# A hybrid encoder step on one Trainium2 core: the sliding window's first weights and columns cast before the gates end, and two scores ahead of the last memory values

## The chip, the cores and the metric

The kernel runs on one core of a Trainium2 chip. A core has five engines that run side by side, each taking its own instructions in order and waiting on semaphores: TensorE (PE, matrix products, with its weight loads shown apart as PEld), VectorE (DVE), ScalarE (ACT), GpSimd (POOL) and SyncE (SP), which here only issues transfers. Any of the last three can also issue transfers, and such an issue stands in that engine's own row of instructions. The metric is the device time of one execution in microseconds; less is better. Three executions of the kernel before took 2241.95, 2242.7 and 2243.11 us, so the median is 2242.7 us.

## The reference

One layer of a chunk-causal streaming encoder is computed for a prompt of 1024 tokens and a sample of 64, which the kernel holds side by side as 1088 columns. Cut to what the change touches:

```python
rq, rk, rv, rg, sq, sk, sv, ga, gb = split(rms_norm(x, g_attn) @ w_in)
ret_o = retention(rq, rk, rv)                       # 4 heads, chunkwise recurrence
a = (rms_norm(ret_o) * silu(rg)) @ w_ret_out        # branch A
# branch B: window of the own chunk of 64 and the two before, 16 heads, 2 key heads
s = sq @ sk.T * 64 ** -0.5 + bias                   # scores, masked
m = maximum(max(s), sink)
e = exp(s - m)
b = (e / (sum(e) + exp(sink - m)) @ sv) @ w_swa_out
x += (sigmoid(ga) * a + sigmoid(gb) * b) @ w_mix_out
mk, mv = (rms_norm(mem, g_mem) @ w for w in (w_mk, w_mv))   # 256 memory tokens, 4 heads
x += cross_attention(rms_norm(x, g_cross), mk, mv)
x += swiglu(rms_norm(x, g_ffn))
```

Everything is float32. The matrix products keep that precision with two parts: an operand is split into a high part (a cast to the engine's shorter format) and a low part (the rest), and a product is the sum of high times high, high times low and low times high.

## The kernel before

Activations lie with the 1024 model columns on partitions, eight blocks of 128, and tokens along the row. Two sets of eight large places in on-chip memory (`rings`, each place 2 x 1088 numbers a partition) hold the split operands of a stage, and are handed on from stage to stage; what doesn't fit goes through DRAM buffers named `d_...`. A weight block arrives by a transfer into a place named `raw`, its high part is cast by ACT (`split`, L123) and its low part subtracted by DVE (L124), both into a place named `wq`. `mm3` (L149 to L151) issues the three matmuls of a split product. The large projections run as a Strassen scheme with seven products per pair of weight blocks instead (L205, L206, L208), whose partial sums DVE collects.

The program is one stream of statements which a scheduler spreads over the engines: it simulates times, and orders each engine's instructions by them, within limits that the code gives (`issue_after`, `high_priority`). Memory comes from pools, and a tile that takes a place used before waits for the last use of that place.

The stages, with their time in the trace of before:

- `project_phase` (to about 816 us): all projections and the retention. It ends with twelve pairs of gate columns: four of `w_ga`, four of `w_rg`, four of `w_gb`. For each half of the tokens DVE adds the last partial sum (L571), multiplies by the norm (L577), ACT applies the sigmoid or silu (L580), and a transfer writes the result to `d_gate`, on ACT's queue for `w_ga` and `w_gb` and on SP's for `w_rg`. Between the pairs come steps of `memory_phase`, the keys and values of the memory tokens for three of the four value heads, whose weights have three places of their own, `mw`.
- `mix_phase` (about 816 to 1024 us): the sliding window, with `w_ret_out` as filler. `swa` goes through 34 half chunks. In a loop step it weighs the values of half i - 1 (L1006), computes the scores of half i + 2 (L948), and transposes the probabilities of half i (`turn`, L990). The softmax of a half lies between: DVE adds the bias and takes maxima (L958 or L961, L963 to L968), ACT takes four exponentials (L970) and one for the sink, DVE inverts the sum, POOL scales (L976). The scores have one PSUM place, so each waits until DVE has read the scores before it. What the window leaves of PE's time is filled by half products of `filler`: the operands `ret` (the gated retention, reloaded from `d_gate` in three column chunks of 384, 384 and 320 and split), the last memory value head (`w_mv[3]`), and then 8 x 3 pieces of `w_ret_out`, each in two halves of 12 matmuls and closed by a multiplication with the gate (L1103). Of these `fill` places four half products after the first scores, none after the second, 40 over the 34 loop steps and 8 at the end.
- then `merge_swa`, the cross attention, and the feed-forward part to the end.

Weights come from one pool with five `wq` places and two `raw` places during `project_phase`, and from a second one with six and two behind it. The operands `ret`, the queries, keys and bias (`swin`) and the weights `w_mv[3]` are all loaded by code that stands behind the projection.

## Time and profile before

| | us |
|---|---|
| median of three runs | 2242.7 (2241.95 to 2243.11) |
| profiled execution, its own time | 2244.47 |
| its span in the trace | 2242.7 |
| PE busy | 2168.9 (97%) |
| DVE busy | 1596.0 (71%) |
| ACT busy | 885.4 (39%) |
| POOL busy | 692.1 (31%) |

The profile's page gives the busy time of each engine, and the granted clock of TensorE over the span (PEclk, mean 0.988 of full speed). Its other views cut the trace: a table of windows gives each engine's busy time in each stretch, with clock and share of the transfer engines; the waits list what an engine's instructions waited for; the timeline of one engine lists its instructions with, in brackets, the idle time ahead of each and what ended it. In the names, `pq<-T,wq 128*128 128x272` is a matmul from `T` and `wq` into `pq`; `x8` counts instructions that lie together, and their busy time may overlap. An engine's queue (SPq, ACTq) is where its transfers are issued; the columns of such a row give the start and the time up to the last of its issues, waits included.

### The profile page before, as it was taken

Reading aid. Unit: us, or ns where it says so; the run is one execution under the profiler, and the core shown is the slowest. Engines: PE = TensorE matmul, PEld = TensorE weight load, DVE = VectorE, ACT = ScalarE, POOL = GpSimd, SP = SyncE. Lnnn points to the kernel's source line nnn. Section 1 sums busy time; section 2 is a strip of 40 time slices with the busy share of each in tenths; the row PEclk is TensorE's granted clock in tenths of the full one; section 3 lists DMA queues with packets and bytes.
Section 4 is the critical chain, followed back from the end, with each engine's and each line's share of the span. In section 5 each row is a group of like instructions: output and inputs, shape, how many; then the busy total and the mean of one; then the engine's idle time right before and its main releaser. Section 6 shows DMA issues by size and latency. Waiting matters only on the chain.

```text
span 2242.7 us, 41756 instructions
## 1 busy us (share of the span) xinstructions
PE 2168.9 (97%) x16434; PEld 2105.3 (94%) x16434; DVE 1596.0 (71%) x2655; ACT 885.4 (39%) x1897; POOL 692.1 (31%) x466
## 2 busy tenths in 40 slices
PE   8899999999999989999999999999999999999986
PEld 8899999999999977779999998999999999999986
DVE  7986878666687667776455556668777677778587
ACT  7333333435444355554133333333323222344243
POOL 1441533342253112220000000014556555434462
PEclk9999999999999999999999999999999999999998
DMA  5533445443445475326443111422333332475233
GB/s 193 163 108 114 118 124 136 133 126 114 167 151 181 150 229 163 114 69 211 132 152 101 64 46 59 138 89 88 121 129 102 102 120 90 147 267 184 85 98 108
DMA packets 182599, 290.86 MB, mean 130 GB/s; under 512 B 40290, under 2 KB 110850, under 8 KB 182402
## 3 DMA queue, kind: packets, MB, share of 16 engines
q1 hardware_dynamic: 177794, 279.26, 39.3%
q10 hardware_dynamic: 4608, 8.91, 1.1%
q8 instruction: 130, 2.13, 0.4%
q14 instruction: 67, 0.55, 0.1%
HBM read 196.95 MB, written 91.16 MB: 128 GB/s over the span
## 4 chain that ended last, share of the span: by engine, by line
PE 79%; DVE 11%; DMA 5%; issue 2%; ACT 2%; POOL 1%; SPq 0%; DVEq 0%; ACTq 0%; POOLq 0%
PE pq L208 15%; PE pq L206 15%; PE pq L205 15%; PE pd L149 8%; PE pd L151 8%; PE pd L150 8%; DVE wq L124 2%; PE pout L1006 1%; DMA hl<-d_op 1%; PE pp L990 1%; PE pss L948 1%; DVE T L124 1%; DVE B L124 1%; DVE xg L1294 1%; DMA qs<-d_qkv 1%
## 5 line engine op out<-in xcount | busy, mean ns | idle before, releaser
L124 DVE TENSOR_TENSOR wq<-raw,wq 128x512 fp32r<-128x512 f32 (+1 forms) x505 | 448.8, 893 | 125.2 <-ACT wq L123 122.0
L123 ACT CAST wq<-raw 128x512 fp32r<-128x512 f32 (+1 forms) x505 | 307.5, 614 | 568.0 <-PE pq L208 259.1
L205 PE MATMUL pq<-T,wq 128*128 128x272 f32 x1832 | 492.9, 289 | 6.8 <-DVE u L252 3.6
L206 PE MATMUL pq<-T,wq 128*128 128x272 f32 x1832 | 493.0, 289 | 0.0
L206 PE MATMUL pq<-B,wq 128*128 128x272 f32 x1592 | 428.9, 289 | 9.1 <-DVE B L124 9.1
L205 PE MATMUL pq<-B,wq 128*128 128x272 f32 x1592 | 427.1, 289 | 0.2 <-ACT B L123 0.2
L208 PE MATMUL pq<-T,wq 128*128 128x272 f32 x1832 | 384.5, 290 | 3.4 <-DVE wq L124 3.4
L183 POOL TENSOR_TENSOR raw<-raw 128x512 f32<-128x512 f32 (+1 forms) x59 | 80.1, 1357 | 897.2 <-DVE rs_r L291 485.7
L205 PEld LDWEIGHTS pq<-T,wq 128*128 128x128 f32 x1832 | 346.1, 189 | 7.9 <-DVE u L252 3.7
L206 PEld LDWEIGHTS pq<-T,wq 128*128 128x128 f32 x1832 | 345.9, 189 | 0.3 <-issue 0.3
L208 PE MATMUL pq<-B,wq 128*128 128x272 f32 x1592 | 333.9, 290 | 0.0
L206 PEld LDWEIGHTS pq<-B,wq 128*128 128x128 f32 x1592 | 300.4, 189 | 11.0 <-DVE B L124 10.7
L205 PEld LDWEIGHTS pq<-B,wq 128*128 128x128 f32 x1592 | 300.2, 189 | 0.9 <-issue 0.4
L208 PEld LDWEIGHTS pq<-T,wq 128*128 128x128 f32 x1832 | 291.2, 190 | 4.6 <-DVE wq L124 3.8
L208 PEld LDWEIGHTS pq<-B,wq 128*128 128x128 f32 x1592 | 252.9, 190 | 0.5 <-issue 0.3
L252 DVE TENSOR_TENSOR u<-pq,u 128x544 f32<-128x544 f32 x177 | 127.6, 721 | 109.7 <-PE pq L208 109.2
L186 POOL TENSOR_TENSOR raw<-raw 128x512 f32<-128x512 f32 (+1 forms) x59 | 85.5, 1449 | 127.3 <-DVE wq L124 124.7
L976 POOL TENSOR_TENSOR t<-t,den 128x768 f32<-128x768 f32 (+2 forms) x34 | 47.9, 1408 | 170.7 <-DVE den L974 44.4
L571 DVE TENSOR_TENSOR stage<-pq,u 128x544 f32<-128x544 f32 x112 | 80.4, 718 | 26.4 <-PE pq L208 25.4
L184 POOL TENSOR_TENSOR raw<-raw 128x512 f32<-128x512 f32 (+1 forms) x59 | 87.3, 1480 | 3.7
L1461 POOL TENSOR_TENSOR y<-u,y 128x544 f32<-128x544 f32 x38 | 62.6, 1656 | 72.6 <-DVE y L1459 50.5
L189 POOL TENSOR_TENSOR raw<-raw 128x512 f32<-128x512 f32 (+1 forms) x59 | 83.3, 1412 | 4.4
(373 smaller groups left out, 4677.0 us busy)
## 6 DMA issues: line engine op xcount, KB each, us to landing
hl<-d_op SPq DMA_DIRECT2D x85, 272.0 KB, 4.6
d_qkv<-stage SPq DMA_DIRECT2D x44, 272.0 KB, 2.3
d_op<-stage SPq DMA_DIRECT2D x44, 272.0 KB, 2.4
d_op<-ht SPq DMA_DIRECT2D x44, 272.0 KB, 3.3
raw<-w_gate SPq DMA_DIRECT2D x22, 512.0 KB, 3.5
raw<-w_up SPq DMA_DIRECT2D x22, 512.0 KB, 3.6
d_gate<-stage ACTq DMA_DIRECT2D x32, 272.0 KB, 2.7
raw<-w_down SPq DMA_DIRECT2D x16, 512.0 KB, 4.2
```

Of the source, the lines that this page charges most:

```text
L123: self.last_cast = self.nc.scalar.copy(hi, src).ins
L124: return self.nc.vector.tensor_tensor(out=lo, in0=src, in1=hi.bitcast(F32), op=ALU.subtract).ins
L149: mm(ps, wh, xh, start=start, stop=False)
L150: mm(ps, wh, xl, start=False, stop=False)
L151: self.last_mm = mm(ps, wl, xh, start=False, stop=stop).ins
L184: tt(out=a21, in0=a21, in1=a22, op=add)
L186: tt(out=a11, in0=a22, in1=a11, op=sub)
L189: tt(out=a12, in0=a12, in1=a11, op=sub)
L205: mm(ps[:, c, :HC], w[:, 0, ks], x[:, 0, cs], start=start, stop=False)
L206: mm(ps[:, c, :HC], w[:, 0, ks], x[:, 1, cs], start=False, stop=False)
L208: self.last_mm = mm(ps[:, c, :HC], w[:, 1, ks], x[:, 0, c * HC:(c + 1) * HC], start=False, stop=stop).ins
L252: add = lambda out, a, b: nc.vector.tensor_tensor(out=out, in0=a, in1=b, op=ALU.add)
```

## The change

It has six parts.

1. One weights pool with five `wq` and two `raw` places serves the whole program. The sixth `wq` place is a pool of its own, opened ahead of the fourth pair of `w_ga`, and used by every sixth operand from there on. For this the pool of the Strassen sums is closed and opened again behind it, and the two pools of the gate and memory stage are opened there and no longer ahead of `w_sk`. `mw` has two places and no longer three.
2. `memory_phase` also loads and splits `w_mv[3]`, ahead of the last gate pairs' end.
3. `begin_swa`, called as the last statement of `project_phase`, issues the loads of keys, first queries and bias, the loads of the first chunk of the `ret` operands, and ACT's casts of these and of `w_ret_out[0]`. Their low parts (`first_low`, 10 subtractions) follow behind the maxima of the second scores.
4. The PSUM pool of the filler is opened from the other end, so that other banks come to the scores.
5. The second scores stand ahead of the memory values. Six half products follow them: four of the values, and the two halves of the first piece of `w_ret_out`. 38 are spread over the loop, 8 follow at the end. The pieces go chunk by chunk for the first two weight blocks, and the second and third chunks of the operands are loaded and split by fours during half products 2, 3, 5 and 7 of `w_ret_out`.
6. The last gate pair's four stores, and the four stores of the last memory values, are issued by POOL. They stood on ACT's queue and on SP's. The queries of chunks 4 to 7 are loaded in loop step 2, no longer with the first scores.

The counts of matmuls, casts, subtractions, exponentials and transfers are the same as before. The diff, cut to its core:

```diff
     def new_op(self):
-        return self.wp.tile([P, 2, 512], F32R, tag="wq", bufs=self.wbufs, name="wq")
+        self.turns += self.sixth is not None
+        if self.turns and self.turns % 6 == 0:
+            return self.sixth.tile([P, 2, 512], F32R, tag="wq", bufs=1, name="wq")
+        return self.wp.tile([P, 2, 512], F32R, tag="wq", bufs=5, name="wq")
...
-                with self.weights(5):
-                    self.project_phase()
-                with self.weights(6):
-                    with self.plain_psum():
...
+                self.left = sctx.enter_context(ExitStack())
+                self.sixth, self.turns = None, 0
+                self.wp = self.left.enter_context(tc.tile_pool(name="weights", bufs=2, reuse_waits="tile"))
+                self.project_phase()
+                with self.plain_psum(side="right"):
...
-        room = lambda: mp.tile([P, 1024], F32, tag="mw", bufs=3, name="mw")
+        room = lambda: mp.tile([P, 1024], F32, tag="mw", bufs=2, name="mw")
...
-        for h in range(H - 1):
+        for h in range(H):
             us = [self.unit(io["w_mv"][h, i], 4, 256, room) for i in range(2)]
+            if h == H - 1:
+                self.first_units = us
+                yield
+                return
...
                 for m in range(0, KT, 2):
-                    store = nc.scalar.dma_start if idx else self.store
+                    if (idx, m) == (1, 6):
+                        fctx.close()
+                        self.sixth = self.left.enter_context(tc.tile_pool(name="sixth", bufs=1, reuse_waits="tile"))
+                        self.sums_pool(ctx)
+                        op = ...
+                        mp = ...
+                        memory = self.memory_phase(mp)
+                    store = nc.gpsimd.dma_start if (idx, m) == (2, KT - 2) else nc.scalar.dma_start if idx else self.store
...
+            next(memory)
+            self.begin_swa()
...
                 pieces = self.filler()
-                yield [pieces] * 4
                 yield []
-                count, steps, done = 48 - 8, 2 * 17, 0
+                yield [pieces] * 6
+                count, steps, done = 48 - 10, 2 * 17, 0
...
+    def begin_swa(self):
...
+        with tc.high_priority():
+            self.tokens(self.kT, 0, "ckT")
+            self.load_queries(self.qTs, 0)
+            for e in range(2):
...
+                self.loaded = self.load(self.bias[e * 64:(e + 1) * 64], src)
+        self.rets = [self.rings[1].tile(f"ret{k}", slot=i) for k, i in enumerate((0, 1, 4, 5, 6, 7, 2, 3))]
+        self.marks = []
+        self.first_loads()
...
+    def first_loads(self):
...
+        raw = self.unit_raw(self.io["w_ret_out"][0], KT)
+        for k in range(KT):
+            a = self.ld()[:, :n]
+            with self.tc.issue_after(after):
+                self.last_operand = self.load(a, self.d_gate[0][k, :, c0:c0 + n])
+            r = self.rets[k][:, :, c0:c0 + n]
+            self.first.append((a, r[:, 0], r[:, 1]))
+            nc.scalar.copy(r[:, 0], a)
+        qs = [self.new_op() for i in range(2)]
+        for i, q in enumerate(qs):
+            a = raw[:, i * 512:(i + 1) * 512]
+            nc.scalar.copy(q[:, 0], a)
+            self.first.insert(i * 5, (a, q[:, 0], q[:, 1]))
...
+    def first_low(self):
+        with self.tc.issue_after(self.marks[-1][0]):
+            for a, hi, lo in self.first:
+                self.nc.vector.tensor_tensor(out=lo, in0=a, in1=hi.bitcast(F32), op=ALU.subtract)
+
+    def later_operands(self, c0, n, ks):
+        a, b = self.marks[-1]
+        with self.tc.issue_after(a), self.tc.issue_after(b):
+            for k in ks:
+                x = self.ld()[:, :n]
+                with self.tc.issue_after(self.last_operand):
+                    self.last_operand = self.load(x, self.d_gate[0][k, :, c0:c0 + n])
+                self.split(x, self.rets[k][:, 0, c0:c0 + n], self.rets[k][:, 1, c0:c0 + n])
...
-            for c0, n in CH:
-                operands(c0, n)
+            ld, rets = self.ld, self.rets
+            self.first_low()
...
-                self.store(self.d_mv[h, :, t, :], o)
-                self.store(io["o_mv"][t * P:(t + 1) * P, h * 256:(h + 1) * 256], o)
+                nc.gpsimd.dma_start(self.d_mv[h, :, t, :], o)
+                nc.gpsimd.dma_start(io["o_mv"][t * P:(t + 1) * P, h * 256:(h + 1) * 256], o)
...
+            order = [(m, c) for c in range(3) for m in range(2)] + [(m, c) for m in range(2, KT) for c in range(3)]
+            halves = [range(4), range(4, KT)]
+            extra = {2: (1, 0), 3: (1, 1), 5: (2, 0), 7: (2, 1)}
+            step = 0
+            for m, c in order:
...
+                for ps in self.pieces(u, rets, c0, n):
+                    if step in extra:
+                        i, j = extra.pop(step)
+                        self.later_operands(*CH[i], halves[j])
+                    step += 1
```

Where this moves instructions, four rows of the program show it. Names carry a tile number, and `swin` tiles 9709 and 9710 of the change are keys and queries, as 9704 and 9705 are before; the change's line numbers differ (L205, L206, L208 are L209, L210, L212, and L948 is L942).

PE before, where the last gate pair ends:

```order
L205 MATMUL pq<-T_304,wq 128x272
L206 MATMUL pq<-T_304,wq 128x272
L208 MATMUL pq<-T_304,wq 128x272 x2
L948 MATMUL pss<-swin_9704,swin_9705 128x64 x4
L149 MATMUL pd<-wq,ms_7465 128x256
L150 MATMUL pd<-wq,ms_7465 128x256
```

PE with the change, at the same place:

```order
L209 MATMUL pq<-T_304,wq 128x272
L210 MATMUL pq<-T_304,wq 128x272
L212 MATMUL pq<-T_304,wq 128x272 x2
L942 MATMUL pss<-swin_9709,swin_9710 128x64 x8
L153 MATMUL pd<-wq,ms_7472 128x256
L154 MATMUL pd<-wq,ms_7472 128x256
```

Eight score matmuls, of two halves, stand where four stood; the 48 matmuls of the memory values follow in both.

DVE before, from the last addition of the gates on (`wq<-raw` are the low parts of `w_mv[3]`):

```order
L571 TENSOR_TENSOR stage_553<-pq,u_9489 128x544
L577 TENSOR_TENSOR stage_553<-stage_553,rstd 128x544
L124 TENSOR_TENSOR wq<-raw,wq 128x512 x4
L961 SCALAR_TENSOR_TENSOR t<-pss,swin_9706 128x2x64 x2
L963 TENSOR_REDUCE nm<-t 128x4
L964 TENSOR_TENSOR nm<-nm,sinks 128x4
L124 TENSOR_TENSOR ret_9758<-swin_9707,ret_9758 128x384
L965 TENSOR_SCALAR nm<-nm 128x4
L124 TENSOR_TENSOR ret_9759<-swin_9707,ret_9759 128x384
L968 TENSOR_TENSOR es<-sinks,nm 128x4
L124 TENSOR_TENSOR ret_9760<-swin_9707,ret_9760 128x384
L124 TENSOR_TENSOR ret_9761<-swin_9707,ret_9761 128x384
```

DVE with the change, from the same addition on:

```order
L577 TENSOR_TENSOR stage_553<-pq,u_9496 128x544
L583 TENSOR_TENSOR stage_553<-stage_553,rstd 128x544
L955 SCALAR_TENSOR_TENSOR t<-pss,swin_9711 128x2x64 x2
L957 TENSOR_REDUCE nm<-t 128x4
L958 TENSOR_TENSOR nm<-nm,sinks 128x4
L959 TENSOR_SCALAR nm<-nm 128x4
L962 TENSOR_TENSOR es<-sinks,nm 128x4
L955 SCALAR_TENSOR_TENSOR t<-pss,swin_9711 128x2x64 x2
L957 TENSOR_REDUCE nm<-t 128x4
L967 TENSOR_TENSOR den<-den,es 128x4
L958 TENSOR_TENSOR nm<-nm,sinks 128x4
L968 RECIPROCAL den<-den 128x4
```

The four subtractions for `w_mv[3]` no longer stand between the gates and the scores' bias addition (L961, now L955); the `ret` subtractions no longer stand among the maxima, but behind the second scores' maxima, two rows further on than the last row shown.

ACT before, from the end of the last gate pair on (L580 is the sigmoid, L666 its store, L970 the exponentials):

```order
L580 ACTIVATE stage_553<-stage_553 128x544
L666 DMA d_gate_83<-stage_553 128x544
L580 ACTIVATE stage_553<-stage_553 128x544
L666 DMA d_gate_83<-stage_553 128x544
L123 CAST wq<-raw 128x512 x4
L123 CAST ret_9758<-swin_9707 128x384
L123 CAST ret_9759<-swin_9707 128x384
L123 CAST ret_9760<-swin_9707 128x384
L970 ACT_TABLE_LOAD
L970 ACTIVATE t,den<-t,nm 128x64 x4
L123 CAST ret_9761<-swin_9707 128x384
L972 ACTIVATE es<-es 128x4
```

ACT with the change, from the sigmoid ahead of the last three on (L586 is the sigmoid, L1075 and L1079 are the casts of `first_loads`, L964 the exponentials):

```order
L1075 CAST ret_9725<-swin_9712 128x384
L1075 CAST ret_9726<-swin_9712 128x384
L586 ACTIVATE stage_553<-stage_553 128x544
L1079 CAST wq<-raw 128x512
L1075 CAST ret_9727<-swin_9712 128x384
L1075 CAST ret_9729<-swin_9715 128x384
L1075 CAST ret_9730<-swin_9715 128x384
L586 ACTIVATE stage_553<-stage_553 128x544
L1079 CAST wq<-raw 128x512
L586 ACTIVATE stage_553<-stage_553 128x544
L964 ACT_TABLE_LOAD
L964 ACTIVATE t,den<-t,nm 128x64 x4
```

The casts of the first operands stand among and ahead of the sigmoids, no longer behind them; the stores are gone, and the exponentials of the first two halves follow directly.

POOL before, from its last sum in the gates on (L976 scales the probabilities):

```order
L184 TENSOR_TENSOR raw<-raw 128x512
L186 TENSOR_TENSOR raw<-raw 128x512
L189 TENSOR_TENSOR raw<-raw 128x512
L976 TENSOR_TENSOR t<-t,den 128x4x64 x2
L976 TENSOR_TENSOR t<-t,den 128x4x128 x2
L976 TENSOR_TENSOR t<-t,den 128x768 x30
```

POOL with the change, at the same place (L970 scales, L676 stores the gates, L1135 and L1136 the memory values):

```order
L190 TENSOR_TENSOR raw<-raw 128x512
L193 TENSOR_TENSOR raw<-raw 128x512
L676 DMA d_gate_83<-stage_553 128x544 x4
L970 TENSOR_TENSOR t<-t,den 128x4x64
L1135 DMA d_mv<-swin_9715 128x256
L1136 DMA o_mv<-swin_9715 128x256
L970 TENSOR_TENSOR t<-t,den 128x4x64
L1135 DMA d_mv<-swin_9715 128x256
L1136 DMA o_mv<-swin_9715 128x256
L970 TENSOR_TENSOR t<-t,den 128x4x128 x2
L970 TENSOR_TENSOR t<-t,den 128x768 x30
```

Four issues of stores stand ahead of the first scaling, two ahead of the second, and two ahead of the third.

More of the change, by code (lines that the diff above doesn't have):

```diff
@@ L890, in swa @@
             mm = nc.tensor.matmul
[L892 to L913 removed]
+            flat, kT, bias, qTs, sinks = self.flat, self.kT, self.bias, self.qTs, self.sinks
+            vT = flat[5][:, :KC]
+            vts = [flat[4][:, i * P:(i + 1) * P] for i in range(17)] + [flat[0][:, KC + i * P:KC + (i + 1) * P] for i in range(3)]
             def keep():
@@ L941, in scores @@
                 ks, j0, nk = keys(c)
[L942 removed]
+                if hf == 0 and c % 4 == 0 and 0 < c < 13:
                     self.load_queries(qTs, c + 4)
@@ L967, in scores @@
                 es = sw.tile([P, 2, 2], F32, tag="es", name="es")
-                nc.vector.tensor_tensor(out=es, in0=snk, in1=nm, op=ALU.add)
+                ready = nc.vector.tensor_tensor(out=es, in0=snk, in1=nm, op=ALU.add).ins
                 for v, i in units:
@@ new lines, in tokens, with ld @@
+    def tokens(self, dst, i, cache):
+        self.load(dst[:, :SEQ], self.d_skv[i, :, :SEQ])
+        self.load(dst[:, SEQ:SEQ + P], self.io[cache])
+        self.load(dst[:, SEQ + P:], self.d_skv[i, :, SEQ:])
+    def ld(self):
+        self.lds.append(self.lds.pop(0))
+        return self.lds[-1]
+    def first_loads(self):
+        nc, (c0, n) = self.nc, CH[0]
+        after, self.first = self.loaded, []
+        raw = self.unit_raw(self.io["w_ret_out"][0], KT)
[11 more added lines that the diff above has]
+            self.first.insert(i * 5, (a, q[:, 0], q[:, 1]))
+        self.first_out = [(q[:, 0, i:i + P], q[:, 1, i:i + P]) for q in qs for i in range(0, 512, P)]
@@ L1062, in filler @@
         if True:
-            def ld():
-                self.lds.append(self.lds.pop(0))
-                return self.lds[-1]
-            rets = self.ring_tiles(1, KT, "ret")
-            def operands(c0, n):
-                after = self.loaded
-                for k in range(KT):
-                    a = ld()
-                    with tc.issue_after(after):
-                        ins = self.load(a[:, :n], self.d_gate[0][k, :, c0:c0 + n])
-                    if c0 == 0:
-                        self.operand_loaded = ins
-                    self.split(a[:, :n], rets[k][:, 0, c0:c0 + n], rets[k][:, 1, c0:c0 + n])
-            for c0, n in CH:
-                operands(c0, n)
+            ld, rets = self.ld, self.rets
+            self.first_low()
             us, h = self.first_units, H - 1
```

100 lines of the change are left out of this document (43 added, 57 removed).

## The prediction

> **What bounds the kernel now.** I read the page first. TensorE is busy for 97% of the span, so a change that leaves its matmuls alone can gain no more than the 74 us in which it is idle, plus what a slow clock costs.
>
> ```profile
> span 2242.7 us, 41756 instructions
> PE 2168.9 (97%) x16434; PEld 2105.3 (94%) x16434; DVE 1596.0 (71%) x2655; ACT 885.4 (39%) x1897; POOL 692.1 (31%) x466
> ```
>
> Then I cut the span at the places that the change touches: gates, the border between gates and window, the rest of the window. The columns are length, then busy time of PE, PEld, DVE, ACT and POOL, PE's clock, the share of the transfer engines, GB/s.
>
> ```profile
> 570.00:815.00 245.00, 245.00 (x1985) 244.52 (x1984) 170.16 (x236) 102.54 (x173) 76.92 (x52) 1.00 0.51 166
> 815.00:861.00 46.00, 31.60 (x193) 25.86 (x191) 34.14 (x84) 31.01 (x98) 5.30 (x5) 0.81 0.80 264
> 861.00:1024.00 163.00, 162.61 (x1151) 126.26 (x1150) 125.79 (x273) 82.00 (x311) 42.56 (x29) 1.00 0.31 97
> ```
>
> On both sides PE is full at full clock. Between them it is busy for 31.60 of 46 us at 0.81 of its clock, which costs 31.60 x 0.19 = 6.0 us more. The idle part is read from PE's timeline, each gap in brackets with what ended it:
>
> ```profile
> 816.74 0.66 PE L948 MATMUL pss<-swin,swin 64*128 64x64 f32 x8 [0.82 <-DVE stage L571]
> 819.29 0.58 PE L149 MATMUL pd<-wq,ms 128*128 128x256 f32 x1 [1.88 <-ACT wq L123]
> ...
> 822.10 0.42 PE L150 MATMUL pd<-wq,ms 128*128 128x256 f32 x1
> 822.31 0.42 PE L151 MATMUL pd<-wq,ms 128*128 128x256 f32 x1
> ...
> 823.22 0.28 PE L151 MATMUL pd<-wq,ms 128*128 128x256 f32 x1
> 823.34 0.28 PE L149 MATMUL pd<-wq,ms 128*128 128x256 f32 x1
> ...
> 826.97 0.66 PE L948 MATMUL pss<-swin,swin 64*128 64x64 f32 x8
> 828.34 0.72 PE L948 MATMUL pss<-swin,swin 64*128 64x128 f32 x8 [0.71 <-DVE t L961]
> 829.93 0.33 PE L925 MATMUL pd<-ident,swin 128*128 128x128 f32 x1 [0.31 <-DMA swin<-d_skv]
> 836.58 0.69 PE L149 MATMUL pd<-ret,wq 128*128 128x384 f32 x1 [6.32 <-ACT wq L123]
> 845.33 0.65 PE L1006 MATMUL pout<-pT,swin 64*64 64x256 f32 x4 [1.00 <-ACT pT L993]
> 850.57 0.65 PE L1006 MATMUL pout<-pT,swin 128*64 128x256 f32 x4 [1.07 <-ACT pT L993]
> 854.22 1.11 PE L990 MATMUL pp<-ident,t 128*128 128x128 f32 x4 [2.15 <-POOL t L976]
> ```
>
> The eight gaps add up to 14.3 us. Nearly half is one wait, 6.32 us, for the cast of `w_ret_out[0]`; 1.88 us is the wait for the cast of `w_mv[3]`. With the clock's 6.0 us the stretch holds 20.3 us, and that is the ceiling of the gain.
>
> The 48 matmuls of the memory values show the clock: they start 0.21 us apart at 822, 0.12 apart at 823. At full rate they take 48 x 0.118 = 5.7 us, and here 826.97 - 819.29 = 7.7, so 2.0 us are lost behind a gap of 1.88. Where the gaps are about 1 us the clock holds, and behind the one of 2.15 it falls:
>
> ```profile
> 845.00:854.00 9.00, 5.68 (x40) 4.08 (x40) 7.11 (x18) 4.90 (x19) 0.91 (x1) 0.97 0.95 294
> 854.00:861.00 7.00, 6.78 (x28) 5.41 (x28) 2.85 (x9) 3.71 (x16) 1.67 (x2) 0.55 0.43 152
> ```
>
> Why are the casts late? Partly by the transfers: SP's queue, after the bias loads, stands for 11.6 us behind stores of the gates that ACT issues, before it gets to the `ret` operands; `w_ret_out[0]` comes behind all that.
>
> ```profile
> SPq L117 <- DMA d_gate<-stage: 11.6, 4, 5.6
> ...
> raw<-w_ret_out SPq DMA_DIRECT2D x4, 512.0 KB, 6.2
> ```
>
> **The change, part by part.** *First weights and columns.* The casts of `w_mv[3]` go into the gate stage, where ACT is busy for 102.54 of 245 us and DVE for 170.16; the four casts and subtractions (4 x 0.55 and 4 x 0.63 us by the rows below) hide there. `w_ret_out[0]` and the first `ret` columns are loaded before the last pair ends, and their stores no longer stand in SP's way. So the waits of 1.88 and 6.32 us lose their cause. What is late next is DVE and ACT:
>
> ```profile
> 815.97 0.72 DVE L571 TENSOR_TENSOR stage<-pq,u 128x544 f32<-128x544 f32 x1 [1.50 <-PE pq L208]
> 816.73 0.72 DVE L577 TENSOR_TENSOR stage<-stage,rstd 128x544 f32<-128x544 f32 x1
> 819.27 2.50 DVE L124 TENSOR_TENSOR wq<-raw,wq 128x512 fp32r<-128x512 f32 x4 [1.82 <-ACT wq L123]
> 821.68 0.48 DVE L961 SCALAR_TENSOR_TENSOR t<-pss,swin 128x128 f32<-128x128 f32 x2
> ...
> 839.18 2.40 DVE L124 TENSOR_TENSOR ret<-swin,ret 128x384 fp32r<-128x384 f32 x5
> ```
>
> *The second scores.* The first scores no longer share banks with the gates' sums, so they start at 815.97 and end at 816.63. The second ones use the same place and wait until DVE has read it: 815.97 + 0.72 + 0.72 + 0.48 = about 818.0. New wait: **1.4 us**. The values then run from about 818.7 to 824.3.
>
> *The low parts.* DVE has ten subtractions to do behind the second maxima. ACT's queue decides when:
>
> ```profile
> 817.48 0.66 ACT L580 ACTIVATE stage<-stage 128x544 f32<-128x544 f32 x1 [2.33 <-DVE stage L577]
> 818.62 2.18 ACT L123 CAST wq<-raw 128x512 fp32r<-128x512 f32 x4 [0.48 <-ACT stage L580]
> 820.70 1.33 ACT L123 CAST ret<-swin 128x384 fp32r<-128x384 f32 x3
> 822.05 1.28 ACT L970 ACT_TABLE_LOAD   x1
> 823.41 0.35 ACT L970 ACTIVATE t<-t,nm 128x64 f32<-128x64 f32 x1
> ...
> 825.15 0.20 ACT L972 ACTIVATE es<-es 128x4 f32<-128x4 f32 x1
> 830.52 0.56 ACT L993 COPY pT<-pp 64x512 f32<-64x512 f32 x1
> ```
>
> Casts of the first columns (0.44 us each) stand between the sigmoids now and push the last of them from 818.1 to about 819.7. The table load (1.28) and the first half's exponentials (about 1.5) end at 822.5, and DVE, which waits for them in its order, then finishes the second maxima and starts the low parts at about 823: two of `wq` at 0.62 and eight of `ret` at 0.48 end at 828.1. PE wants the first at 824.3 and uses eight column blocks in 24 matmuls, by their width 0.118 x 384 / 256 = 0.177 us each, 4.2 us, so it keeps just ahead of being starved. I take **0.5 us**; bounds are 0 and 4 us (all ten finished first, as if in one wait).
>
> *The steps behind.* ACT and DVE take their queues in order. Casts of `w_ret_out[2]` stand ahead of the first two copies of transposed probabilities (0.56 us each), and their load can start only when the low part of `w_ret_out[0]` has freed its place, at about 825.5; with the 6.2 us to land of such loads it is there at about 831.7, when PE already wants the copy. By laying these queues end to end I get six waits in loop steps 0 to 4: 0.65, 0.55, 1.7, 0.7, 0.35 and 0.65, **4.6 us** together. The nearest rows are the waits of 1.00 and 1.07 for the same copies, and 2.15 for POOL, so half of the sum and double of it are the bounds.
>
> *The third column chunk.* Its eight casts and subtractions go into two loop steps each time four. A step without them is 4.9 us long, from one weighing to the next:
>
> ```profile
> 891.35 1.23 PE L1006 MATMUL pout<-pT,swin 128*64 128x256 f32 x8
> ...
> 896.26 1.23 PE L1006 MATMUL pout<-pT,swin 128*64 128x256 f32 x8
> ```
>
> Of such a step DVE is busy for 4.9 x 125.79 / 163 = 3.8 us (the window from 861 to 1024); with 4 x 0.48 it is 5.7. ACT comes to 4.9 x 82.00 / 163 + 4 x 0.44 = 4.2 and stays below. I take 0.9 for each of two steps, **1.8 us**; bounds 0 and 4, the latter if four steps are held up by 1 us.
>
> *The clock.* One of the new waits is near 1.9, so I take one loss as with the values, **2.0 us**; bounds 0 and 6.0, today's. The Trainium skill ("TensorE: Matmul & The Clock Gate", Part 1) says that the clock halves after an idle window of about 3.4 us; by that no new wait would reach it, the term would be 0 and the sum 12.0. The trace disagrees: here gaps of 1.88 and 2.15 us were enough, and the measurement decides.
>
> *The rest* I cost at nothing. The sixth weight place and two instead of three `mw` places touch the gate stage, whose PE has no idle microsecond to hide a stall, but the last `mw` load leaves well ahead of its casts:
>
> ```profile
> L123 ACT CAST wq<-mw x28: 603/621/625, 682.7 to 788.7; 128x512 fp32r<-128x512 f32 x28
> ...
> L117 SPq DMA_DIRECT2D mw<-w_mv x6: 328/328/333, 725.0 to 776.1; - x6
> ...
> DMA to landing us min/median/max: 3.4/4.4/8.1
> ```
>
> The eight stores on POOL's queue I take at the 0.33 us of ACT's issues, since POOL is busy for 5.30 of the 46 us; before shows no issue by POOL, so this is only the nearest row.
>
> ```profile
> 818.17 0.35 ACTq L666 DMA_DIRECT2D d_gate<-stage  x1
> ```
>
> **The sum.** 20.3 - 1.4 - 0.5 - 4.6 - 1.8 - 2.0 = 10.0 us gained. The profiled execution would go from 2244.47 to 2234.5; it stands 1.8 above the median of the runs, and against that median it is 2242.7 - 10.0 = 2232.7.
>
> **Rivals.** *The full gain.* ACT and DVE keep up: only the 1.4 and half of the 4.6 us remain, the clock holds. 20.3 - 3.7 = 16.6, so 2226. For it: from 861 on the same kind of step runs with 0.39 us of idle in 163. Against: ACT and DVE are busy for 31 and 34 of the 46 us already.
>
> *The waits only move.* The casts stand earlier in ACT's order, but wait for places that the last gate products still read, and hold up sigmoids and exponentials; the waits behind double to 9.2, the third chunk costs 4, the low parts 2, and the clock stays as it is for half of its cost, 3.0. 20.3 - 1.4 - 2 - 9.2 - 4 - 3.0 = 0.7, about 2242; halfway to my sum it is 2237. For it: the transfers run at 0.80 of their capacity there, and the loads of `w_ret_out[2]` sit in the middle. Against: two more half products (4.2 us of PE work) are now in front of the steps that wait.
>
> *Slower by POOL's queue.* Four stores stand ahead of the first scaling of probabilities, two ahead of the second and two ahead of the third. With q us for an issue, the first is hidden up to about 9 (one issue after the last sigmoid; the transpose wants it at 829.8), the third up to about 3, since four issues lie between 825 and the transpose at about 838. Beyond that each us costs 4. It eats the whole gain at q = 3 + 10/4 = 5.5, and at q = 7 the time is 2242.7 - 10 + 16 = 2249. For it: nothing in this trace, which has no such issue. Against: the nearest issues take 0.33. The Trainium skill ("SBUF — State Buffer", the box on DVE blocking DMA) says that transfers issued by GpSimd need descriptors written by its cores, which DVE can lock out for as long as it runs some of its operations; no run here shows it yet.
>
> *Slower by the gate stage.* With two `mw` places each of the last loads starts up to one unit later. The last load has 788.7 - 776.1 = 12.6 us, less 0.6 for the first of its two casts, less 4.4 to land: 7.6 us of slack. A stall of 2.5 us beyond that in six loads would cost 15, and the time would be 2248.
>
> **How the numbers follow.** Less than 0.2% (4.5 us) is about what can't be told from no change in this kernel, so faster means below 2238.2 and slower above 2247.2. My sum has 0.48, the full gain 0.14, the moved waits 0.26, POOL's queue 0.06 and the gate stage 0.06. My sum and the full gain are faster, and of the moved waits somewhat under half: 0.73. The moved waits' rest is the same: 0.15. Slower: 0.12. The range reaches from 2223, beyond the full gain with half of its waits gone, to 2243, the end of the moved waits; beyond it lie the two slower cases and a little of the others, 0.17.
>
> **What would show it.** In the profile after, PE's wait for the `w_ret_out` cast of 6.3 us and that for the `w_mv` cast of 1.9 us are gone, and a wait of about 1.4 us for DVE stands ahead of the second scores. SP's wait of 11.6 us for the gates' stores is gone. The stretch from the last gate matmul to the point of equal work is shorter by about 10 us, with waits for `pT` of up to 1.7 us and a clock of above 0.9. PE stays at 245 of 245 us in the gates and full behind 861. I am wrong if the gates show idle PE, if a scaling by POOL ends a wait of over 3 us, or if ACT's queue holds PE for more than 5 us at one place.

## The result, and the profile after

The changed kernel takes 2245.76 us in the median of 22 runs (2240.55 to 2253.35), beside 2242.93 us for the kernel before in 22 runs. The ratio is 1.0019 (95% interval 1.0012 to 1.0027): 0.19% slower, where 0.45% faster was forecast. The profiled execution has a span of 2246.3 us.

The places that the prediction spoke of look much as it said. PE's timeline of the changed kernel between gates and window, gaps in brackets:

```profile
821.28 0.66 PE L942 MATMUL pss<-swin,swin 64*128 64x64 f32 x8 [1.47 <-DVE t L955]
838.41 0.65 PE L1000 MATMUL pout<-pT,swin 64*64 64x256 f32 x4 [2.32 <-ACT pT L987]
839.80 0.72 PE L942 MATMUL pss<-swin,swin 64*128 64x128 f32 x8 [0.74 <-DVE t L955]
850.21 0.65 PE L1000 MATMUL pout<-pT,swin 128*64 128x256 f32 x4 [1.31 <-ACT pT L987]
851.91 0.66 PE L984 MATMUL pp<-ident,t 128*128 128x128 f32 x4 [0.20 <-POOL t L970]
857.95 1.97 PE L984 MATMUL pp<-ident,t 128*128 128x128 f32 x8 [1.60 <-POOL t L970]
...
875.00 0.65 PE L1000 MATMUL pout<-pT,swin 64*64 64x256 f32 x4 [1.54 <-DVE pT L989]
882.04 1.09 PE L984 MATMUL pp<-ident,t 128*128 128x128 f32 x8 [0.49 <-POOL t L970]
```

The waits of 1.88 and 6.32 us for casts are gone, and the second scores wait 1.47 us for DVE. But the table of windows (length, then busy time of PE, PEld, DVE, ACT and POOL, PE's clock, the share of the transfer engines, GB/s) shows idle time where there was none or less: 1.75 us in the gates, which were full, 2.42 us behind 861 us, where it was 0.39, and 10.56 us in the last feed-forward group:

```profile
570.00:815.00 245.00, 243.25 (x1962) 242.07 (x1962) 168.21 (x238) 104.27 (x177) 76.20 (x53) 1.00 0.53 170
815.00:861.00 46.00, 38.26 (x257) 33.01 (x256) 35.36 (x83) 28.48 (x93) 9.06 (x12) 0.93 0.77 245
861.00:1024.00 163.00, 160.58 (x1135) 123.90 (x1135) 127.09 (x277) 83.41 (x315) 43.53 (x29) 1.00 0.33 101
2128.00:2200.00 72.00, 61.44 (x439) 60.79 (x438) 59.97 (x65) 27.74 (x50) 45.61 (x33) 0.88 0.27 81
```

The last row of before's, for the same 72 us, in which PE is idle for 5.73:

```profile
2128.00:2200.00 72.00, 66.27 (x512) 65.40 (x510) 60.35 (x73) 30.61 (x56) 45.19 (x33) 0.95 0.34 102
```

In the gates PE now waits twice, and in the last group three times. The changed kernel:

```profile
669.77 0.40 PE L209 MATMUL pq<-T,wq 128*128 128x272 f32 x1 [0.86 <-DVE u L256]
...
683.35 0.39 PE L209 MATMUL pq<-T,wq 128*128 128x272 f32 x1 [0.89 <-ACT u L259]
...
2149.13 0.59 PE L209 MATMUL pq<-T,wq 128*128 128x272 f32 x1 [3.02 <-DVE y L1513]
...
2178.02 0.59 PE L209 MATMUL pq<-T,wq 128*128 128x272 f32 x1 [4.47 <-ACT wq L123]
...
2194.52 0.39 PE L209 MATMUL pq<-T,wq 128*128 128x272 f32 x1 [3.07 <-ACT wq L123]
```

Before has no wait in the gates, and shorter ones in the last group:

```profile
2159.99 0.39 PE L205 MATMUL pq<-T,wq 128*128 128x272 f32 x1 [0.83 <-ACT wq L123]
...
2173.46 0.39 PE L205 MATMUL pq<-T,wq 128*128 128x272 f32 x1 [1.54 <-DVE B L124]
...
2177.41 0.82 PE L208 MATMUL pq<-T,wq 128*128 128x272 f32 x2 [3.18 <-DVE wq L124]
```

To compare whole stages I cut both traces at the same instructions of PE, by their starts: the last transposition of the retention's output, the last gate product, the first product with `swa` operands, the first scores of the cross attention, the last transposition of the roots (the inverse norms) ahead of the feed-forward part, and the first product with `wb` near the end. Each kernel was profiled twice (the second time as e7 and e8 below):

| us, first and second profile | before | changed | difference of the means |
|---|---|---|---|
| up to the gates | 577.9, 577.5 | 578.9, 577.4 | +0.4 |
| gates | 237.7, 237.7 | 240.0, 240.9 | +2.8 |
| window with filler | 223.4, 221.7 | 216.7, 217.6 | -5.4 |
| merge | 205.0, 203.0 | 205.1, 205.0 | +1.1 |
| cross attention and its output | 276.4, 276.3 | 273.9, 274.0 | -2.4 |
| feed-forward | 678.5, 680.7 | 690.5, 691.0 | +11.2 |
| last products to the end | 43.7, 43.8 | 41.2, 40.7 | -2.8 |

In these two pairs the window gained about half of what was forecast, and the gates and the feed-forward part, which were costed at nothing, gave back more. Not all of the feed-forward row is the last group: up to the same matmul at about 2120 us the two pairs already differ by 3.0 and 1.5 us, 2.2 and 0.6 of it in a slower clock at the start of the part (last section).

### The profile page after: what moved, and what is told of

Same layout as the page of the kernel before. It is cut to its first block, busy times and chain, and to the rows that moved or that the text cites. A ratio compares the mean times of both kernels' runs of the same rounds, so it can differ in the third digit from the quotient of the medians.

```text
span 2246.3 us, 41741 instructions
## 1 busy us (share of the span) xinstructions
PE 2177.0 (97%) x16434; PEld 2113.0 (94%) x16434; DVE 1611.3 (72%) x2655; ACT 883.7 (39%) x1897; POOL 704.4 (31%) x474
## 5 line engine op out<-in xcount | busy, mean ns | idle before, releaser
L124 DVE TENSOR_TENSOR wq<-raw,wq 128x512 fp32r<-128x512 f32 (+1 forms) x499 | 458.4, 923 | 152.5 <-ACT wq L123 149.9
L123 ACT CAST wq<-raw 128x512 fp32r<-128x512 f32 (+1 forms) x499 | 303.0, 613 | 565.1 <-PE pq L212 202.4
L209 PE MATMUL pq<-T,wq 128*128 128x272 f32 x1832 | 495.6, 290 | 16.6 <-ACT wq L123 7.5
L210 PE MATMUL pq<-T,wq 128*128 128x272 f32 x1832 | 495.1, 290 | 0.0
L210 PE MATMUL pq<-B,wq 128*128 128x272 f32 x1592 | 430.4, 290 | 7.8 <-DVE B L124 7.8
L209 PE MATMUL pq<-B,wq 128*128 128x272 f32 x1592 | 427.9, 289 | 0.2 <-ACT B L123 0.2
L212 PE MATMUL pq<-T,wq 128*128 128x272 f32 x1832 | 384.9, 291 | 0.0
L209 PEld LDWEIGHTS pq<-T,wq 128*128 128x128 f32 x1832 | 348.2, 190 | 18.2 <-ACT wq L123 8.0
L187 POOL TENSOR_TENSOR raw<-raw 128x512 f32<-128x512 f32 (+1 forms) x59 | 78.6, 1333 | 909.9 <-DVE rs_r L295 482.7
L210 PEld LDWEIGHTS pq<-T,wq 128*128 128x128 f32 x1832 | 347.9, 190 | 0.3 <-issue 0.3
L212 PE MATMUL pq<-B,wq 128*128 128x272 f32 x1592 | 334.6, 290 | 0.0
L210 PEld LDWEIGHTS pq<-B,wq 128*128 128x128 f32 x1592 | 301.4, 189 | 9.9 <-DVE B L124 9.6
L209 PEld LDWEIGHTS pq<-B,wq 128*128 128x128 f32 x1592 | 301.2, 190 | 1.1 <-issue 0.4
L212 PEld LDWEIGHTS pq<-T,wq 128*128 128x128 f32 x1832 | 292.5, 191 | 0.8 <-issue 0.8
L212 PEld LDWEIGHTS pq<-B,wq 128*128 128x128 f32 x1592 | 253.8, 191 | 0.5 <-issue 0.3
L190 POOL TENSOR_TENSOR raw<-raw 128x512 f32<-128x512 f32 (+1 forms) x59 | 87.4, 1482 | 129.4 <-DVE wq L124 126.9
L193 POOL TENSOR_TENSOR raw<-raw 128x512 f32<-128x512 f32 (+1 forms) x59 | 86.9, 1473 | 16.6 <-DVE wq L124 13.0
L970 POOL TENSOR_TENSOR t<-t,den 128x768 f32<-128x768 f32 (+2 forms) x34 | 48.8, 1434 | 136.8 <-DVE den L968 62.1
L188 POOL TENSOR_TENSOR raw<-raw 128x512 f32<-128x512 f32 (+1 forms) x59 | 88.6, 1501 | 3.6
```

What stands on the lines that cost most here:

```text
L123: self.last_cast = self.nc.scalar.copy(hi, src).ins
L124: return self.nc.vector.tensor_tensor(out=lo, in0=src, in1=hi.bitcast(F32), op=ALU.subtract).ins
L187: tt(out=a11, in0=a11, in1=a21, op=sub)
L188: tt(out=a21, in0=a21, in1=a22, op=add)
L190: tt(out=a11, in0=a22, in1=a11, op=sub)
L193: tt(out=a12, in0=a12, in1=a11, op=sub)
```

## The experiments

Theory A: the weights pool in two pieces costs the time, in the gates and at the far end. Its rival, theory B: those losses are one execution's luck, and the window gained less than it seems. Kernels that ran side by side share their runs of the kernel before.

**The pools alone (e1, e2).** e1 is the kernel before with part 1 of the change; e2 adds to it that one pool of six places is opened behind the projection.

```diff
# e1: before, with new_op, the weights pool, the sixth pool, mw and the late op and mp pools of the change
# e2: e1 and
                 self.project_phase()
+                self.six_places(sctx)
+    def six_places(self, ctx):
+        self.left.close()
+        self.sixth, self.turns, self.wbufs = None, 0, 6
+        self.wp = ctx.enter_context(self.tc.tile_pool(name="weights6", bufs=2, reuse_waits="tile"))
```

> The kernel before with part 1 of the change alone: one weights pool of five places plus the sixth in a pool of its own, two mw places, the sums pool closed and opened again and the op and mp pools opened ahead of the fourth w_ga pair. Loads, casts, scores and stores stay as before. Theory A (the pools cost at the far end: the order of the last feed-forward group changes with the split weights pool): about 6 to 7 us slower than before, 2249, with the loss of about 2 us in the gates between 660 and 690 us and 5 to 6 us behind 2130 us, and nothing gained between 815 and 861. Theory B (the slow end of the change's profile is one execution's luck, and the window gained less than its profile shows): within 2 us of before.

> As e1_pools, but behind the projection the five places and the sixth are closed and one pool of six places is opened, as before has it. The order of instructions behind 1024 us is then the one of before on every engine. Theory A: the far end is as before, so only the gates' loss stays: 1 to 3 us slower than before, about 2245. Theory B: the same as e1_pools within 1 us.

e1 took 2249.83 us beside 2241.82: ratio 1.0039 (1.0026 to 1.0052). e2 took 2242.98: 1.0009 (0.9999 to 1.0018). The gates took 240.7 and 240.2 us; the feed-forward part with the end took 727.8 in e1 and 719.6 in e2, where before took 722.2 and 724.5. So part 1 alone makes the kernel 8 us slower, and nearly 7 of them come from keeping the pool in two pieces behind the projection. Theory A stands. One thing was not expected: the window took 219.1 us in e1 and 218.4 in e2, though the loads, casts and scores there are before's, on ACT and DVE in a somewhat different order.

**One pool of six again, later (e3, e4).** The changed kernel, with `six_places` ahead of the feed-forward part (e3) or of the cross attention (e4).

```diff
# e3
+                self.six_places(sctx)
                 self.ffn_phase()
# e4
+                    self.six_places(sctx)
                     self.cross_phase()
```

> The changed kernel, but ahead of the feed-forward phase the five places and the sixth are closed and one pool of six places is opened. PE's and POOL's order behind that is the one of before. Theory A: the 5 to 6 us of the far end come back, 2239 to 2241, which is 2 to 4 us faster than before. Theory B: no difference to the changed kernel, 2245 to 2247.

> As e3_six_ffn, but the one pool of six places is opened ahead of the cross attention. Theory A: as e3_six_ffn, 2239 to 2241, or 3 us more if the 3 us that the changed kernel gains at 1390 to 1400 us in its profile belong to the split pool. Theory B: no difference to the changed kernel.

Both missed theory A's 2239 to 2241: 2246.62 us (1.0015, 1.0004 to 1.0027) and 2244.36 us (1.0011, 1.0000 to 1.0022). The feed-forward part is short again, 678.4 and 677.7 us, as theory A has it, but the seam, where one pool closes and the next opens, costs much of it: the stretch from the last cross scores to the roots took 129.1 us in e3, where the changed kernel took 123.1 and 123.3, and the merge took 210.5 in e4, where it took 205. In e3 PE waits there 2.22 and 1.03 us for the high and the low parts of the next stage's first weights; in e4 it waits 2.16 us for DVE, and that late weights are behind this is argued, not shown. e4's window is long too, 222.3 us, in an order of instructions that is the changed kernel's. e3's one profile is 4.6 us shorter than the changed kernel's two, and its twelve runs don't show that; this was not followed up.

**The phase of the sixth place (e5), and the wait for a load (e6).** By the program, one pool of six places and "five and every sixth" differ where operands are not given back in the order in which they were taken, as in the last group. e5 puts the count forward by 3 there, which restores before's order on PE and POOL without a seam. e6 also keeps casts and subtractions of later `w_ret_out` weights behind the first copies of probabilities. In the changed kernel those casts stood ahead of them, and ACT waited for a load:

```profile
836.58 1.14 ACT L123 CAST wq<-raw 128x512 fp32r<-128x512 f32 x2 [7.08 <-DMA raw<-w_ret_out]
837.63 0.26 ACT L921 COPY swin<-pd 128x128 f32<-128x128 f32 x1
837.78 0.58 ACT L987 COPY pT<-pp 64x512 f32<-64x512 f32 x1
```

```diff
# e5
     def down(self, starts):
         nc, io = self.nc, self.io
+        self.turns += 3
# e6: e5 and
                 if m not in units:
-                    units[m] = self.unit(io["w_ret_out"][m], KT)
+                    with tc.issue_after(self.turned[-1]), tc.issue_after(self.marks[4][0]):
+                        units[m] = self.unit(io["w_ret_out"][m], KT)
# turned: the first three copies of transposed probabilities on ACT
```

> The changed kernel, with one statement more at the start of the last projection of the feed-forward part: the count of weight operands, by which every sixth goes to the sixth place, is put forward by 3. No pool is closed. PE's and POOL's order behind 1024 us is then the one of before. Theory A (which operands the sixth place holds in the last group sets the order there, and this costs 5 to 9 us): 6 to 7 us faster than the changed kernel, 2238 to 2240, with the stretch from the gain of the norm at about 1520 to the first of the last products some 8 to 12 us shorter than in the changed kernel. Theory B (the time in the last group is luck of one execution): no difference to the changed kernel.

> As e5_shift, and the casts and subtractions of the third and later w_ret_out weights are issued behind the third copy of transposed probabilities (ACT) and the fifth half's maxima (DVE), so that ACT's wait of 7.1 us for the third load no longer stands ahead of the first copies. Theory A (this wait is what keeps PE waiting in the first loop steps): PE's waits of 2.3 and 0.7 us at about 838 and 840 us shrink to under 1 together, 2 to 4 us faster than e5_shift, about 2236. Theory B (the waits only move, to later casts or to DVE): within 1 us of e5_shift.

e5 took 2241.44 us beside 2242.51 (0.9996, 0.9986 to 1.0005), 4.3 us under the changed kernel, where 6 to 7 were expected; its feed-forward part with the end took 722.6 us, where the changed kernel's took 731.7 both times. e6 took 2235.83 us (0.9973, 0.9961 to 0.9985), 5.6 us under e5, where 2 to 4 were expected. PE's timeline of e6 at the place:

```profile
819.97 0.66 PE L942 MATMUL pss<-swin,swin 64*128 64x64 f32 x8 [1.48 <-DVE t L955]
829.34 0.44 PE L154 MATMUL pd<-ret,wq 128*128 128x384 f32 x1 [1.13 <-DVE ret L1089]
846.75 0.65 PE L1002 MATMUL pout<-pT,swin 128*64 128x256 f32 x4 [1.30 <-ACT pT L987]
850.57 0.66 PE L984 MATMUL pp<-ident,t 128*128 128x128 f32 x4 [2.32 <-POOL t L970]
```

The waits of 2.32 and 0.74 us are gone, as theory A has it, and a part came back behind them (1.13 for a low part, and 2.32 for POOL in place of 0.20 and 1.60). In the two profiles e6's window is 3.0 us shorter than e5's (215.2 and 218.2 us); where the rest of the 5.6 us comes from was not followed up.

**Both kernels once more (e7, e8).** No edit; one profile each.

> The kernel before, profiled once more. Theory A (the profiled execution of before was slower between gates and window than most): the stretch from the last gate product to the first product behind the window takes 217 to 220 us where it took 223.4, with PE idle for 10 to 12 us where it was 14.8. Theory B (it was typical): 222 to 224 again.

> The changed kernel, profiled once more. Theory A: gates again 2.4 us longer than before (240 where it was 237.7), the stretch of the window 215 to 218, and the last group again 6 to 12 us longer than before. Theory B (luck): at least one of the three differs by more than 3 us from the first profile.

The table above has the stages. For before neither theory was met: the window took 221.7 us. For the changed kernel the gates, the window and the feed-forward part with the end came out again within 1 us, so the losses are not luck.

**Parts of part 1 (e9, e10), and parts 5 and 6 undone (e11, e12).**

```diff
# e9: before, with fctx.close(), the sums pool again and op and mp opened at (1, 6)
# e10: before, with
-        room = lambda: mp.tile([P, 1024], F32, tag="mw", bufs=3, name="mw")
+        room = lambda: mp.tile([P, 1024], F32, tag="mw", bufs=2, name="mw")
# e11: the changed kernel, with
-                yield []
-                yield [pieces] * 6
-                count, steps, done = 48 - 10, 2 * 17, 0
+                yield [pieces] * 4
+                yield []
+                count, steps, done = 48 - 8, 2 * 17, 0
# e12: the changed kernel, with nc.gpsimd.dma_start replaced by nc.scalar.dma_start (gates) and self.store (values)
```

> The kernel before; only the sums pool is closed and opened again, and the op and mp pools are opened there, ahead of the fourth w_ga pair, as the change does it. Three mw places, no sixth place in the gates, and two weights pools as before. Theory A (the late opening shifts the memory work's loads and crowds DVE between 660 and 690 us): the gates take 240 us again where before took 237.7 (both profiles), with PE waiting for DVE or ACT near 669 and 683 us. Theory B (two mw places or the sixth place do it): 237.7.

> The kernel before with two mw places and no other edit. Theory A: the gates take 237.7 us as before. Theory B (a memory weight comes late with two places): 239 to 241. The window of before took 223.4 and 221.7 us in its two profiles, and 218 to 219 in the two kernels with part 1 alone; if the freed mw place is the reason, it is 218 to 219 here.

> The changed kernel with the old order of the scores: four half products (the memory values) behind the first scores, none behind the second, 40 over the loop. Theory A (the second scores in front of the values bring part of the window's gain, by giving ACT and DVE their work earlier): the window's stretch takes 219 to 222 us, where it takes 216.7 to 218.2 in the changed kernel. Theory B (the gain is all from earlier loads and casts): 216.5 to 218.5.

> The changed kernel with the last gate pair's stores on ACT's queue and the last memory values' stores on SP's, as before. Theory A (SP stood behind the gates' stores, and this move is needed): SP waits for the gates' stores again for some 10 us behind 808, the ret columns arrive later, and the window's stretch takes 219 to 222 us. Theory B (POOL's issues of 0.55 us cost as much as they save): 216 to 218 us.

e9 and e10 have gates of 237.7 us: neither the late pools nor two `mw` places alone lengthen them. Their windows took 219.6 and 219.7 us. As e9's order of instructions in the window is before's on every engine, and e10's but for three of SP's, the window of before varies by itself: 223.4, 221.7, 219.6, 219.7, with a mean of 221.1. The changed order varies as much: 216.7 and 217.6 in the changed kernel, 216.6 in e3, 222.3 in e4 and 218.2 in e5, with a mean of 218.3.

e11's and e12's windows took 219.3 and 219.4 us. Both lie at the low end of theory A's range, but 1 us above that mean is less than either spread, and each is one profile; I leave both open. Among SP's waits behind 795 us in e12 the gates' stores do not appear, so the wait of 11.6 us goes without the move too, and the reason that I gave for the move is not what it shows.

**The sixth place later, and one number (e13, e14).** Both are e6 with the sixth place taken into use from the first `w_gb` pair on. They differ in the number by which the count is put forward.

```diff
+                    if (idx, m) == (2, 0):
+                        self.sixth = sixth        # its pool is opened at (1, 6), as in the change
...
+        self.turns += 2        # e13; 5 in e14
```

> As e6_shift_act, but the sixth place is taken into use only from the first w_gb pair on (its pool is opened where it was); the count is put forward by 2 and no longer 3, which gives before's order of PE and POOL in the last group. Theory A (the sixth place lets casts run ahead while the memory work begins, and this crowds DVE): the gates take 237.7 to 238.2 us, and the kernel is 2 us faster than e6_shift_act, about 2233.5 to 2234.5. Theory B (the late pools and two mw places together do it): the gates take 240 again and the time is e6_shift_act's, 2236.

> As e13_sixth_later, with one number changed: the count is put forward by 5 and no longer 2, which gives the changed kernel's order of PE and POOL in the last group. Theory A (the place of the sixth operand alone costs the time there): 6 to 8 us slower than e13_sixth_later. Theory B (the last group's time depends on what comes before it): within 2 us of it.

e13 took 2232.80 us (2230.62 to 2233.35) beside 2241.36: ratio 0.9957 (0.9945 to 0.9970). e14 took 2241.19: 0.9996 (0.9987 to 1.0005). Both have gates of 237.7 us, in which PE doesn't wait, and every profile with the early use has the two waits (0.86 to 1.55 us each). So the early use of the sixth place, together with the rest of part 1, is what lengthens them; that DVE is crowded by casts run ahead was argued, not measured apart. And one number costs 8.4 us. The two profiles differ by 10.5 us behind the roots, of which 3.6 stand ahead of 2120 us, mostly the clock again; the last group holds 6.9. In e13 PE waits in the last group as before does:

```profile
2148.98 0.39 PE L209 MATMUL pq<-T,wq 128*128 128x272 f32 x1 [0.65 <-ACT wq L123]
...
2162.47 0.39 PE L209 MATMUL pq<-T,wq 128*128 128x272 f32 x1 [1.54 <-DVE B L124]
2166.41 0.82 PE L212 MATMUL pq<-T,wq 128*128 128x272 f32 x2 [3.18 <-DVE wq L124]
```

In e14 it waits as in the changed kernel's second profile, which has 2.46, 2.64, 3.36 and 3.35 us:

```profile
2144.44 0.40 PE L209 MATMUL pq<-T,wq 128*128 128x272 f32 x1 [2.46 <-DVE y L1519]
...
2157.41 0.60 PE L209 MATMUL pq<-T,wq 128*128 128x272 f32 x1 [2.46 <-ACT wq L123]
...
2173.39 0.39 PE L209 MATMUL pq<-T,wq 128*128 128x272 f32 x1 [3.10 <-ACT wq L123]
...
2189.85 0.39 PE L209 MATMUL pq<-T,wq 128*128 128x272 f32 x1 [3.41 <-ACT wq L123]
```

The casts that PE waits for are late because their load is. ACT and SP of e14:

```profile
2149.79 0.51 ACT L123 CAST wq<-raw 128x384 fp32r<-128x384 f32 x1 [7.99 <-DMA raw<-w_down]
...
2146.56 14.91 SPq L117 DMA_DIRECT2D raw<-w_down  x4
```

The same of e13:

```profile
2138.75 0.51 ACT L123 CAST wq<-raw 128x384 fp32r<-128x384 f32 x1 [3.74 <-DMA raw<-w_down]
...
2135.30 18.19 SPq L117 DMA_DIRECT2D raw<-w_down  x4
```

The first of these four loads leaves 11 us later in e14, right behind the end of a subtraction into `wq` (DVE, L124, 2146.49 us). The casts ahead of it are late as well: at the start of the group ACT's casts into `wq` stand 11.0 us apart in e14 (2123.86 and 2134.86 us), with ten casts of operands `T` and `B` between them, and 4.5 us in e13 (2119.99 and 2124.53), with three between. By the program a load waits for a `raw` place, which its casts and subtractions give back, these wait for `wq` places, and in e14 the sixth place goes to an operand that is still held there; no view shows a place, so this step is argued.

## Why the prediction was wrong

- "The rest I cost at nothing" is the step that failed. It looked at the sixth place and at `mw` only in the gates, and took PE to stay full behind 861 us without giving a reason. The instructions are the same there, their order is not: the feed-forward part with the end became 9.5 and 7.2 us longer in the two pairs of profiles, of which 6.4 and 5.7 in the last group, and e13 against e14 puts 8.4 us on the phase of the sixth place alone.
- The same step in the gates, with "7.6 us of slack" for the `mw` loads: right for `mw` (e10 shows no loss), wrong for the sixth place, which I didn't cost. It is 2.8 us. Idle PE in the gates was one of the signs of being wrong that I had named.
- The window's 10.0 us were 5.4 in two pairs of profiles, and 2.8 if all profiles with the same order are taken (means of 221.1 and 218.3), which is within the spread of either order. As the window is as short with part 1 alone (e1, e2), no run shows that the earlier loads and casts made it shorter as the changed kernel has them. With ACT's order mended it is shorter: 215.2, 215.9 and 213.5 us in e6, e13 and e14, 6 us under before's mean. The ceiling of 20.3 was read from one execution, whose window is 2.3 us over the mean of four.
- Of the new waits, 1.4 us for the second scores measured 1.47; the third chunk's 1.8 measured 1.54 + 0.49 = 2.0; the low parts' 0.5 don't show; the waits in the loop steps, 4.6, measured 2.32 + 0.74 + 1.31 + 0.20 + 1.60 = 6.2. For the first two of these the cause was the one named, ACT held by the third load of `w_ret_out`: e6 takes it away, they go, and it is 5.6 us faster than e5.
- The clock's 2.0 us measured 38.26 x 0.07 = 2.7 in the stretch up to 861. That a gap near 1.9 us brings one such loss is not a rule: the last section has one wait with and without it.
- The waits that move: SP's wait for the gates' stores is gone as foreseen (e12 shows that it goes without the move as well), and POOL's issues took more than the 0.33 us assumed, but hide:

```profile
819.80 0.55 POOL L676 DMA_DIRECT2D d_gate<-stage  x1 [11.72 <-ACT stage L586]
822.09 0.54 POOL L676 DMA_DIRECT2D d_gate<-stage  x1 [1.74 <-ACT stage L586]
...
828.41 0.58 POOL L1135 DMA_DIRECT2D d_mv<-swin  x1 [1.52 <-ACT swin L1134]
```

  The rival of POOL's queue falls with that: its price was to decide from 5.5 us an issue on. The Trainium skill's box on DVE blocking DMA ("SBUF — State Buffer") finds nothing to hold on to here: seven of the eight issues took 0.54 to 0.58 us and the first 0.71, and the one with DVE idle beside it (at 823.16 us) took 0.54 like those with DVE at work. The box speaks of some operations of DVE; whether one of them ran beside an issue was not tested.
- The cross attention's 2.4 us gain was not foreseen. There before's PE waits 0.49, 1.48 and 0.73 us between 1390 and 1398 us, and the changed kernel's does not. The stage takes 276.4 us in e1 and e2 and 273.3 in e11 and e12, so neither part 1 nor the order of the scores nor the stores' queues is what brings it; which of the other parts does was not tested.

The slower outcome did come, but from neither of the two mechanisms that the prediction gave for it. The gates' rival had the right stage and the wrong part of the edit.

## What to carry to other kernels

A change in how places are handed out reaches every later stage that uses the pool: compare the whole order of instructions, and cost each stage in which it differs, also where the diff touches nothing. Where operands are not given back in the order they were taken, a pool in two pieces with a fixed turn is not a pool of the same size; which operand gets the odd place is worth trying (e13 beats both kernels, by 0.43% the one before). And a ceiling or a gain read from one execution should be checked against further profiles, stage by stage: here one stage with one order of instructions took from 216.6 to 222.3 us.

## What the runs showed of the hardware

The same gap can cost or not. Both kernels wait for 2.05 us for the roots ahead of the feed-forward part; behind it before's profile keeps the clock and the changed kernel's does not (rows of before and after):

```profile
1520.00:1530.00 10.00, 9.49 (x76) 9.30 (x77) 10.00 (x17) 7.67 (x13) 2.76 (x1) 1.00 0.01 2
```

```profile
1514.00:1527.00 13.00, 12.48 (x81) 12.19 (x80) 11.59 (x17) 7.91 (x14) 3.38 (x3) 0.76 0.01 2
```

That is 12.48 x 0.24 = 3.0 us between two executions, of the size of the whole result. All sixteen profiles have this wait, 2.04 to 2.06 us long. In the 13 us from its end on the clock is 1.00 in nine of them, 0.87 in four (e7, e9, e10, e11) and 0.74 in three (the changed kernel twice, and e14). The Trainium skill ("TensorE: Matmul & The Clock Gate", Part 1) calls the window that decides on the clock free-running; these rows agree with that. The same part lets the clock fall after an idle window of about 3.4 us; here a wait of 2.05 us stood ahead of it, and the measurement decides.
